# Two-layer hybrid decoder trunk: a third down block by Strassen's scheme, its weight sums partly on GpSimd, and the stick-breaking norm ahead of the query up-projection

## Chip, cores and metric

The kernel runs on one core of one Trainium2 chip. The metric is the time of one execution on the device, in microseconds (us). A core has TensorE (PE in the profile; its weight loads are PEld), VectorE (DVE), ScalarE (ACT), GpSimd (POOL) and SyncE (SP), which here only issues DMAs. PE writes its results to PSUM, eight banks of 128x512 f32; everything else lies in SBUF.

## The reference

256 tokens of width 1024 pass through two layers. A layer has two half-step SwiGLU feed-forwards (width 2816), between them a token mixer of two attention groups side by side, and at the end a gated input embedding. Cut to what matters:

```
h = h + 1/2 * swiglu(rms_norm(h))                     # silu(x Wg) * (x Wu), then Wd: 2816 -> 1024
u = norm(h) @ w_in                                    # sb q, k, v | q latent | kv latent | rope key
sb  = rms_norm(stick_breaking(q, k, v))               # 8 heads of 64
mla = rms_norm(softmax attention from the latents)    # q = norm(c_q) @ w_uq, kv = norm(c_kv) @ w_ukv
h = h + concat(sb, mla) @ w_out
h = h + 1/2 * swiglu(rms_norm(h))
h = h + sigmoid(norm(h) @ Wg) * (p[i] @ Wp)
```

All of it is in f32. The kernel gets near f32 accuracy from three matmuls on a rounded format: each operand is split into a high part (a rounded copy) and a low part (the rest), and high x high, high x low and low x high are summed (`mm3`, L220 to L225, lines L222, L223, L224 of the profile).

## The kernel before

**Weights.** Every weight comes once from HBM in pieces of 128x1024 f32 (512 KB), in the order of use. A piece passes four stations: a DMA from SP into one of six `raw` buffers, a rounded copy by ScalarE into one of six `wh` buffers (L132), the subtraction raw - wh by VectorE into one of six `wl` buffers (L133), and PE. So the splitting of a piece can start only when PE has done with the piece six places ahead. A plain piece of the feed-forward feeds 12 matmuls of 512 columns.

**Feed-forward (`ffn`, L470).** The 2816 inner columns are five blocks of 512 (0 to 4) and one of 256 (5). Gate and up products are made block by block; ScalarE makes the silu (L475), VectorE multiplies (L479), PE transposes (L450, tile `ft`) and both engines split the result into `f` (L455, L456). Which moment the transposes take in PE's order is set by a small planner: `soon` puts a step off by so many us of estimated PE time, `tick` runs what is due, `flush` runs all.

Then comes the down projection into four banks `d`. A plain block is 48 matmuls. Blocks 1 and 2 (`SEVEN`, L32) use Strassen's scheme in Winograd's form on a 2x2 split of the block: seven products of six matmuls instead of eight, 42 in place of 48. Its left operands are sums of the gated activations (`sums`, L410, made when the block's transposes are done: four VectorE sums and a split). Its right operands are sums of the four 128x1024 weight quarters b11, b12, b21, b22. In `Seven.operands` (L179) all four sums are made in place by VectorE (`add`, L169, tile `raw`, line L170), and each of the seven operands is copied by ScalarE (L175) and subtracted by VectorE (L176). The order is: the plain block 0 (two weight units, `head`), Strassen block 1, the plain block 5, Strassen block 2, then eight VectorE steps that combine the banks and add them to h (L559 to L567), and the plain blocks 3 and 4 (`lagging`, L365), in which the second half of the tokens runs three chunks behind the first, so that the first half's residual, norm and transposes lie beside the second half's matmuls.

**Mixer (`mix`, L573).** Stick-breaking attention of four head pairs (`sb_scores`, `sb_tail`, `sb_values`) is interleaved with the input projections. At the end the order on PE is: `sb_values(2)`, the query up-projection `uq` (48 matmuls of 256 columns, L716 to L720), `sb_values(3)`, then the norm of the stick-breaking output (`token_norm`, L724: squares by ScalarE, logarithm and exponential for the square root, five VectorE steps, result `on_sb`), `kn` and `vm`, the two MLA score steps, the transposes of `on_sb` (`turned`, L739, tile `yt_sb`), whose split gives the operand `y0h`, `y0l` (layer 0; `y1` in layer 1), and the output projection `wo` (L845 on), which begins with these. GpSimd has one product for the rope key (L685) and three for the query's rope (L758, L759, L765) in each layer, and nothing else of weight.

**Order on the engines.** The framework sorts the instructions of each engine by its own estimate of when they are ready, with the program's order as priority, and hands out buffers in the same way; on the chip each engine runs its list strictly in order.

Of the kernel before, what the change touches and what calls it, by code (L numbers as in the profile page):

```python
# [17 lines left out]
P = 128  # L18
T = 256
# [9 lines left out]
WARM = 11  # L29


SEVEN = (1, 2)  # L32

F_TAGS = ("sbq", "sbk", "v", "vm", "n0h", "n0l", "n1h", "n1l", "f4h", "f4l", "f5h", "f5l")

# [10 lines left out]
def trunk(ctx: ExitStack, tc: tile.TileContext, xT, xr, pT, w, gains, fgain, consts, out):  # L46
# [41 lines left out]
    def load_consts():  # L88
        c = tp.tile([P, 768], F32, tag="w2", name="c")[:, : 5 * P]
        after(nc.sync.dma_start(c, consts[:, 0 : 5 * P]), newest_load[0])  # L90
        after(nc.sync.dma_start(c_sb[:, P:], consts[:, C_FOLD:]), newest_load[0])
        nc.vector.tensor_copy(c_r, c)
# [16 lines left out]
    class Unit:  # L109


        def __init__(self, nk, cols=None, sub=1, cut=1, again=None):
            self.u = at[0] if again is None else again.u
            at[0] += again is None
            self.cols = cols or UNIT // nk
            self.per = max(1, PIECE // self.cols)
            self.sub, self.cut = sub, cut
            self.parts, self.here = {}, set()
# [35 lines left out]
    class Seven:  # L154

        def __init__(self):
            self.u = at[0]
            at[0] += 2  # L160
            self.raw = {}

        def load(self, i):
            r = raw_p.tile([P, PIECE], F32, tag="raw", name=f"raw7_{self.u}_{i}")
            newest_load[0] = nc.sync.dma_start(r, w[self.u + i // 2, :, i % 2 * PIECE : (i % 2 + 1) * PIECE])
            self.raw[i] = r
            return r

        def add(self, i, j):  # L169
            nc.vector.tensor_tensor(self.raw[i], self.raw[i], self.raw[j], ALU.add)  # L170

        def parts(self, i):
            r, name = self.raw[i], f"{self.u}_{i}_{next(ids)}"
# [5 lines left out]
        def operands(self):  # L179

            b11, b12, b21, b22 = range(4)
            self.load(b11)
            yield 1, self.parts(b11)
            self.load(b22)
            yield 3, self.parts(b22)
            self.load(b12)
            self.add(b11, b12)
            yield 5, self.parts(b11)
            self.load(b21)
            yield 2, self.parts(b21)  # L190
            self.add(b12, b22)
            yield 7, self.parts(b12)
            self.add(b11, b22)
            yield 6, self.parts(b11)
            self.add(b11, b21)
            yield 4, self.parts(b11)


    due = []
# [27 lines left out]
    def both(x, *ix):  # L227
        return tuple(t[ix] for t in x)
# [161 lines left out]
    class Gates:  # L390
# [19 lines left out]
        def sums(self, i):  # L410

            a, b = self.turned[i, 0], self.turned[i, 1]
            lo, hi = slice(0, 2), slice(2, 4)
            e = SEVEN.index(i)
            out = tuple(f_p.tile([P, 4, T], F32R, tag=f"s{e}{q}", name=f"s{q}_{self.tag}_{i}") for q in "hl")
            two = [wt(f"w{2 + k}", f"sum{k}_{self.tag}_{i}") for k in range(2)]
            s1, s2, s3, s4 = (two[k // 2][:, k % 2].rearrange("p (a b) -> p a b", a=2) for k in range(4))
            nc.scalar.copy(s3, b[:, lo])
            nc.vector.tensor_tensor(s1, s3, b[:, hi], ALU.subtract)
            nc.vector.tensor_tensor(s2, s1, a[:, lo], ALU.subtract)  # L420
            nc.vector.tensor_tensor(s3, a[:, lo], s3, ALU.subtract)
            nc.vector.tensor_tensor(s4, s2, a[:, hi], ALU.add)
            for k in range(2):
                sh, sl = both(out, slice(None), slice(2 * k, 2 * k + 2))
                nc.scalar.activation(sh, two[k], AF.Copy)
                nc.vector.tensor_tensor(sl, two[k], sh.bitcast(F32), ALU.subtract)
            self.s[i] = out
# [42 lines left out]
    def ffn(x, n, tag, gcol, between=None, feed=None):  # L470
# [13 lines left out]
        for i in range(NBLK):  # L484
            last = i == NBLK - 1
            g = [bank(f"g_{tag}_{i}{t}") for t in range(2)]
            sub = {"sub": 2} if feed and i == 0 else {}
            wg = wide([Unit(4, **sub) for _ in range(2)])
            if last:
                for k in range(KC):  # L490
                    for t in range(2):
                        tok_mm(g[t], wg, x, t, (k,))
                for t in range(2):
                    silu, rest = gated(i, t, g[t][:, 0:T], g[t][:, T : 2 * T], T)
                    rest()
                logs_after(silu)
                continue
            u = [bank(f"u_{tag}_{i}{t}") for t in range(2)]
            wu = wide([Unit(4, **sub) for _ in range(2)])
            if i == 0 and feed:  # L500
                for k in range(KC):
                    if k % 2 == 0:
                        feed(k // 2)
                    for o, w_of in ((g, wg), (u, wu)):
                        for t in range(2):
                            tok_mm(o[t], w_of, x, t, (k,))
                feed(4)
                first = [g, u]
                continue
            else:  # L510
                if i == 0:
                    tok_mm(g[0], wg, x, 0)
                    flush()
                    tok_mm(g[1], wg, x, 1)
                else:
                    for k in range(KC):
                        for t in range(2):
                            tok_mm(g[t], wg, x, t, (k,))
                if i == 1 and feed:
                    load_consts()  # L520
                    for t in range(2):
                        gated(0, t, first[0][t], first[1][t])[1](4.5)
                rests = [gated(i, t, g[t], u[t])[1] for t in range(2)]
                for k in range(KC):
                    for t in range(2):
                        tok_mm(u[t], wu, x, t, (k,))
            for r in rests:
                r()
        d = four(f"d_{tag}")

        def block(i):

            us = [Unit(2) for _ in range(2 if i < NBLK - 1 else 1)]
            return [(us[k // 2], k % 2, 4 * i + k) for k in range(2 * len(us))]
# [3 lines left out]
                for t in range(2):  # L538
                    down_mm(d, u, j, gates(k), gates.at(k), t, first and c == 0, False)

        head = block(0)
        plain(head[:2], True)
        flush()
        plain(head[2:])

        p = {2: d[0][0], 3: d[0][1], 4: d[1][0]}
        p.update((i, bank(f"p{i}_{tag}")) for i in (1, 5, 6, 7))
        own = (1, 5, 6, 7)
        for i in SEVEN:
            seven_mm(p, gates.seven(i), Seven().operands(), lambda q: q in own and i == SEVEN[0], lambda q: q in own and i == SEVEN[-1])  # L550
            if i == SEVEN[0]:
                plain(block(NBLK - 1))

        def to_h(t, f, src):
            c = half(f)
# [11 lines left out]
        to_h(1, 1, b)  # L567
        if between is not None:
            between()
        rest = [c for i in range(1, NBLK - 1) if i not in SEVEN for c in block(i)]  # L570
        return lagging(rest, d, gates, 0.5, tag, gcol, 3, False)

    def mix(x, n, L, g0):  # L573
# [136 lines left out]
        nc.tensor.matmul(f[:, :T], fold, krt, start=True, stop=True)  # L710
        kr = at_p.tile([P, T], F32, tag="kr", name=f"kr{L}")
        nc.vector.tensor_copy(kr, f[:, :T])
        sb_values(2)


        u = Unit(2)  # L716
        qs = [pair(f"uq{L}_{i}") for i in range(4)]
        for m in range(8):
            for k in range(2):
                mm3(qs[m // 2][:, m % 2], u.at(k, m * P, (m + 1) * P), both(xq, slice(None), k), k == 0, k == 1)  # L720

        sb_values(3)

        def token_norm(src, name):  # L724

            ss = tp.tile([P, 2], F32, tag="tss", name=f"tss_{name}")
# [12 lines left out]
        def turned(o, c0, gcol, name, parts=(0, 1)):  # L739

            for i in parts:
# [5 lines left out]
                for j in range(2):  # L747
                    c = 2 * i + j
                    split(y, a[:, j], c0 + c, gcol + c, name)

        y = new_x(f"y{L}")
        on = token_norm(ov, f"sb{L}")

        qn = at_p.tile([P, 4, T], F32, tag="sbq", name=f"qn{L}")
        for i in range(2):
# [62 lines left out]
        def mla_values(hp):  # L818
            pt = st["t", hp]
            for e in range(2):  # L820
# [3 lines left out]
                nc.tensor.matmul(om[1][:, c], pt[:, e, P:T], vm[:, 0, c], start=hd == 0, stop=True, skip_group_check=True)  # L824
                nc.tensor.matmul(om[1][:, c], pt[:, e, T:W], vm[:, 1, c], start=False, stop=True, skip_group_check=True)

        mla_scores(0)
        mla_scores(1)
        mla_probs(0)
        turned(on, 0, g0 + G_SB, f"sb{L}")  # L830
        mla_probs(1)
        nc.vector.reciprocal(ri, sm)
        d = four(f"wo{L}_")
# [141 lines left out]
def _weights(i):  # L975
# [9 lines left out]
    for L in range(DEPTH):  # L985
# [5 lines left out]
        def ffn(n):  # L991
            wg, wu, wd = (i[f"{n}_w_{s}"][L] for s in ("gate", "up", "down"))
            for j in range(NBLK - 1):
                m = ar(512 * j, 512 * j + 512)
                wide(wg, m)
                wide(wu, m)
            m = ar(DFF - 256, DFF)
            wide(np.concatenate([wg[:, m], wu[:, m]], axis=1), ar(512))

            def down(b):  # L1000
                units.extend(cols(wd[k : k + 256], ar(DM)) for k in range(512 * b, min(512 * b + 512, DFF), 256))

            down(0)
            for b in SEVEN:
                for k in (512 * b, 512 * b + 256):
                    units.append(np.concatenate([cols(wd[k : k + 256], ar(c, c + 512)) for c in (0, 512)], axis=1))
                if b == SEVEN[0]:
                    down(NBLK - 1)
            for b in range(1, NBLK - 1):
                if b not in SEVEN:  # L1010
                    down(b)
# [81 lines left out]
```

## Time and profile before

| | |
|---|---|
| three runs | 1039.70, 1041.15, 1043.06 us; median 1041.15 us |
| the profiled execution, by the clock of the runs | 1042.18 us |
| its span in the trace (first to last instruction) | 1040.3 us |
| busy: PE, PEld, DVE, ACT, POOL | 1019.1, 858.3, 714.9, 602.7, 7.3 us |
| mean granted PE clock | 0.992 |
| instructions | 13749, of them 5130 matmuls |
| read from HBM | 185.45 MB |

Times in the trace count from the span's start. A matmul's row shows its own duration from start to end; matmuls overlap in the array, so what one costs is the distance between two starts, and the rows below are used in that way. "idle before <- X" names what ended an engine's wait. Layer 0's first feed-forward (`a0` here, tiles `_a`) has its down projection from 132 to 191 us, its mixer follows until 300 us; the second feed-forward (`b0`) has its down projection from about 430 us. Layer 1 repeats this some 513 us later.

### The profile page before, as it was taken

To read this page: it belongs to the slowest core of one execution; us is meant where nothing else is said; L and a number is where in the kernel's file an instruction comes from. 1 tells how busy PE (TensorE), PEld (TensorE's weight loads), DVE (VectorE), ACT (ScalarE), POOL (GpSimd) and SP (SyncE) were. 2 spreads that over 40 slices of the span, in tenths; PEclk is the share of its full clock that TensorE was granted. 3 is DMA by queue.
4 is the path that set the end of the run, shared out by engine and by line. 5 is a ranking of instruction groups with operands and counts; after the bars stand their busy time and mean duration, and the time that the engine had idled before them with its cause. 6 is when DMAs were issued, how large, how long until landed. Compare 5 with 4: busy or idle time off the path is not lost.

```text
span 1040.3 us, 13749 instructions
## 1 busy us (share of the span) xinstructions
PE 1019.1 (98%) x5130; PEld 858.3 (82%) x5130; DVE 714.9 (69%) x991; ACT 602.7 (58%) x921; POOL 7.3 (1%) x13
## 2 busy tenths in 40 slices
PE   9999999999899999999999999999998999999996
PEld 8878888899788888877888888889997888888785
DVE  5676578866576665788875656888675756657975
ACT  5945455766565554555764555456855745545564
POOL 0000000000000000000000000000010000000000
PEclk9999999999899999999999999999999999999998
DMA  8865545763236555357565554476533365553551
GB/s 299 310 214 183 181 138 186 244 212 133 81 127 209 186 184 185 122 189 244 167 218 183 182 186 158 141 258 222 189 102 101 136 218 189 185 183 121 190 205 41
DMA packets 53490, 187.39 MB, mean 180 GB/s; under 512 B 6064, under 2 KB 6192, under 8 KB 53424
## 3 DMA queue, kind: packets, MB, share of 16 engines
q1 hardware_dynamic: 52992, 185.95, 53.1%
q8 instruction: 40, 0.66, 0.3%
q10 hardware_dynamic: 432, 0.57, 0.2%
q14 instruction: 26, 0.21, 0.1%
HBM read 185.45 MB, written 1.05 MB: 179 GB/s over the span
## 4 chain that ended last, share of the span: by engine, by line
PE 79%; DVE 9%; ACT 6%; issue 3%; DMA 2%; SPq 0%; ACTq 0%; DVEq 0%
PE g_b L224 4%; PE g_b L222 4%; PE g_b L223 4%; PE u_b L223 3%; PE u_b L224 3%; PE u_b L222 3%; PE g_a L224 3%; PE g_a L222 3%; PE g_a L223 3%; PE u_a L222 3%; PE u_a L223 3%; PE u_a L224 3%; DVE wl L176 3%; DVE raw L170 2%; PE d_a L223 2%
## 5 line engine op out<-in xcount | busy, mean ns | idle before, releaser
L133 DVE TENSOR_TENSOR wl<-raw,wh 128x1024 fp32r<-128x1024 f32 (+1 forms) x322 | 382.8, 1198 | 220.0 <-ACT wh L132 217.7
L132 ACT ACTIVATE wh<-raw 128x1024 fp32r<-128x1024 f32 (+1 forms) x322 | 330.1, 1037 | 251.8 <-PE u_b L224 50.2
L175 ACT ACTIVATE wh<-raw 128x1024 fp32r<-128x1024 f32 x56 | 58.0, 1057 | 63.5 <-DVE raw L170 37.3
L176 DVE TENSOR_TENSOR wl<-raw,wh 128x1024 fp32r<-128x1024 f32 x56 | 67.5, 1223 | 30.8 <-ACT wh L175 30.2
L223 PE MATMUL d_b<-wl,fh_b 128*128 128x512 f32 x128 | 50.7, 396 | 3.3 <-DVE wl L133 2.2
L223 PE MATMUL d_a<-wl,fh_a 128*128 128x512 f32 x128 | 50.0, 393 | 0.8 <-DVE wl L176 0.8
L224 PE MATMUL d_b<-wh,fl_b 128*128 128x512 f32 x128 | 50.0, 390 | 0.0
L224 PE MATMUL d_a<-wh,fl_a 128*128 128x512 f32 x128 | 49.6, 390 | 0.0
L222 PE MATMUL d_a<-wh,fh_a 128*128 128x512 f32 x128 | 49.0, 394 | 0.0
L222 PE MATMUL d_b<-wh,fh_b 128*128 128x512 f32 x128 | 48.4, 394 | 0.0
L170 DVE TENSOR_TENSOR raw<-raw,raw 128x1024 f32<-128x1024 f32 x32 | 39.1, 1221 | 0.6
L222 PE MATMUL g_a<-wh,x0h 128*128 128x512 f32 x96 | 38.5, 403 | 0.0
L222 PE MATMUL g_b<-wh,x_mix0h 128*128 128x512 f32 x96 | 38.4, 400 | 0.0
L222 PE MATMUL g_b<-wh,x_mix1h 128*128 128x512 f32 x96 | 38.4, 400 | 0.0
L222 PE MATMUL g_a<-wh,xe0h 128*128 128x512 f32 x96 | 38.4, 400 | 0.0
L224 PE MATMUL g_a<-wh,xe0l 128*128 128x512 f32 x96 | 37.6, 391 | 0.0
L224 PE MATMUL g_b<-wh,x_mix1l 128*128 128x512 f32 x96 | 37.5, 390 | 0.0
L224 PE MATMUL g_b<-wh,x_mix0l 128*128 128x512 f32 x96 | 37.5, 390 | 0.0
L223 PE MATMUL g_b<-wl,x_mix0h 128*128 128x512 f32 x96 | 37.4, 390 | 0.0
L223 PE MATMUL g_b<-wl,x_mix1h 128*128 128x512 f32 x96 | 37.4, 390 | 0.0
L223 PE MATMUL g_a<-wl,xe0h 128*128 128x512 f32 x96 | 37.4, 390 | 0.0
L223 PE MATMUL g_a<-wl,x0h 128*128 128x512 f32 x96 | 37.4, 391 | 0.0
(452 smaller groups left out, 2516.7 us busy)
## 6 DMA issues: line engine op xcount, KB each, us to landing
raw<-in_w SPq DMA_DIRECT2D x338, 512.0 KB, 4.1
raw<-in_w SPq DMA_DIRECT2D x16, 256.0 KB, 4.6
xin<-in_xT SPq DMA_DIRECT2D x4, 256.0 KB, 4.9
h<-in_xr SPq DMA_DIRECT2D x2, 512.0 KB, 7.9
p<-in_pT SPq DMA_DIRECT2D x2, 256.0 KB, 6.2
fg<-in_fgain SPq DMA_DIRECT2D x1, 512.0 KB, 7.1
out_h<-hg SPq DMA_DIRECT2D x2, 256.0 KB, 2.3
out_h<-hg ACTq DMA_DIRECT2D x2, 256.0 KB, 2.7
```

What stands on the lines that cost most here:

```text
L132: nc.scalar.activation(wh[:, a], r[:, a], AF.Copy),
L133: nc.vector.tensor_tensor(wl[:, a], r[:, a], wh[:, a].bitcast(F32), ALU.subtract),
L170: nc.vector.tensor_tensor(self.raw[i], self.raw[i], self.raw[j], ALU.add)
L175: newest_wh[0] = nc.scalar.activation(wh, r, AF.Copy)
L176: nc.vector.tensor_tensor(wl, r, wh.bitcast(F32), ALU.subtract)
L222: nc.tensor.matmul(o, ah, bh, start=start, stop=False, **kw)
L223: nc.tensor.matmul(o, ah, bl, start=False, stop=False, **kw)
L224: newest_mm[0] = nc.tensor.matmul(o, al, bh, start=False, stop=stop, **kw)
```

## The change

Four edits. (1) Block 3 joins the Strassen blocks. The order becomes: half of block 0, Strassen 1, the other half of block 0, Strassen 2, block 5, Strassen 3, the combination, block 4. (2) Of the four weight sums of a Strassen block two go to GpSimd (b12 + b22, and b11 + that sum), two stay on VectorE. The products are taken in the order 1, 3, 2, 7, 6, 5, 4. The activation sums of blocks 1 and 2 lie in one of the two x buffers, those of block 3 in the buffers `s0h`, `s0l`, which block 1 used before. The weights of block 4 are asked for ahead of the combination (`u.ready()`). (3) In the mixer `sb_values(3)` and the norm come before `uq`, and the transposes of `on_sb` before the MLA scores. (4) In the very first feed-forward the silu of block 0 is ordered behind the exponential of the second token half's norm.

```diff
-SEVEN = (1, 2)
+SEVEN = (1, 2, 3)
...
+        def sum(self, eng, o, a, b, op=ALU.add):
+            eng.tensor_tensor(self.raw[o], self.raw[a], self.raw[b], op)
...
             self.load(b11)
             yield 1, self.parts(b11)
+            self.load(b12)
             self.load(b22)
+            self.sum(nc.gpsimd, b12, b12, b22)
             yield 3, self.parts(b22)
-            self.load(b12)
-            self.add(b11, b12)
-            yield 5, self.parts(b11)
+            self.sum(nc.gpsimd, b11, b11, b12)
             self.load(b21)
             yield 2, self.parts(b21)
-            self.add(b12, b22)
             yield 7, self.parts(b12)
-            self.add(b11, b22)
             yield 6, self.parts(b11)
-            self.add(b11, b21)
-            yield 4, self.parts(b11)
+            self.sum(nc.vector, b22, b11, b22, ALU.subtract)
+            yield 5, self.parts(b22)
+            self.sum(nc.vector, b21, b11, b21)
+            yield 4, self.parts(b21)
...
+            if e == 0:
+                self.spare = tuple(x_p.tile([P, KC, T], F32R, tag=f"x{q}", name=f"sx{q}_{self.tag}") for q in "hl")
+            if e < 2:
+                out = both(self.spare, slice(None), slice(4 * e, 4 * e + 4))
+            else:
+                out = tuple(f_p.tile([P, 4, T], F32R, tag=f"s0{q}", name=f"s{q}_{self.tag}_{i}") for q in "hl")
...
+                    exp = newest[0]
                     for t in range(2):
-                        gated(0, t, first[0][t], first[1][t])[1](4.5)
+                        silu, r = gated(0, t, first[0][t], first[1][t])
+                        after(silu, exp)
+                        r(4.5)
...
         plain(head[:2], True)
         flush()
-        plain(head[2:])
...
-            if i == SEVEN[0]:
-                plain(block(NBLK - 1))
+            if i != SEVEN[-1]:
+                plain(head[2:] if i == SEVEN[0] else tail)
+
+        rest = [c for i in range(1, NBLK - 1) if i not in SEVEN for c in block(i)]
+        for u, _, _ in rest[::2]:
+            u.ready()
...
-        sb_values(2)
-        u = Unit(2)
-        qs = [pair(f"uq{L}_{i}") for i in range(4)]
-        for m in range(8):
-            for k in range(2):
-                mm3(qs[m // 2][:, m % 2], u.at(k, m * P, (m + 1) * P), both(xq, slice(None), k), k == 0, k == 1)
-        sb_values(3)
...
+        sb_values(2)
+        sb_values(3)
         y = new_x(f"y{L}")
         on = token_norm(ov, f"sb{L}")
+        u = Unit(2)
+        qs = [pair(f"uq{L}_{i}") for i in range(4)]
+        for m in range(8):
+            for k in range(2):
+                mm3(qs[m // 2][:, m % 2], u.at(k, m * P, (m + 1) * P), both(xq, slice(None), k), k == 0, k == 1)
...
+        turned(on, 0, g0 + G_SB, f"sb{L}")
         mla_scores(0)
         mla_scores(1)
         mla_probs(0)
-        turned(on, 0, g0 + G_SB, f"sb{L}")
```

The packing of the weights follows the new order.

More of the change, by code (lines that the diff above doesn't have):

```diff
@@ L163, in load @@
         def load(self, i):
[L164 to L170, printed above, removed]
+            self.raw[i] = raw_p.tile([P, PIECE], F32, tag="raw", name=f"raw7_{self.u}_{i}")
+            newest_load[0] = nc.sync.dma_start(self.raw[i], w[self.u + i // 2, :, i % 2 * PIECE : (i % 2 + 1) * PIECE])
+        def sum(self, eng, o, a, b, op=ALU.add):
+            eng.tensor_tensor(self.raw[o], self.raw[a], self.raw[b], op)
         def parts(self, i):
@@ L414, in sums @@
             e = SEVEN.index(i)
-            out = tuple(f_p.tile([P, 4, T], F32R, tag=f"s{e}{q}", name=f"s{q}_{self.tag}_{i}") for q in "hl")
+            if e == 0:
[4 more added lines that the diff above has]
+                out = tuple(f_p.tile([P, 4, T], F32R, tag=f"s0{q}", name=f"s{q}_{self.tag}_{i}") for q in "hl")
             two = [wt(f"w{2 + k}", f"sum{k}_{self.tag}_{i}") for k in range(2)]
@@ L539, in plain @@
                     down_mm(d, u, j, gates(k), gates.at(k), t, first and c == 0, False)
-        head = block(0)
+        head, tail = block(0), block(NBLK - 1)
         plain(head[:2], True)
         flush()
-        plain(head[2:])
         p = {2: d[0][0], 3: d[0][1], 4: d[1][0]}
@@ L569, in ffn @@
             between()
-        rest = [c for i in range(1, NBLK - 1) if i not in SEVEN for c in block(i)]
         return lagging(rest, d, gates, 0.5, tag, gcol, 3, False)
@@ L1003, in ffn @@
             down(0)
+            down(NBLK - 1)
             for b in SEVEN:
@@ L1006, in ffn @@
                     units.append(np.concatenate([cols(wd[k : k + 256], ar(c, c + 512)) for c in (0, 512)], axis=1))
-                if b == SEVEN[0]:
-                    down(NBLK - 1)
             for b in range(1, NBLK - 1):
```

## The prediction

> **What bounds the kernel now.** I read the page first, then the waits of PE, then the stages in which PE waits (windows and timeline).
>
> ```profile
> PE 1019.1 (98%) x5130; PEld 858.3 (82%) x5130; DVE 714.9 (69%) x991; ACT 602.7 (58%) x921; POOL 7.3 (1%) x13
> ...
> PEclk9999999999899999999999999999999999999998
> ```
>
> PE is busy nearly all the time, and its granted clock falls below full in one slice in the middle (the eleventh, 260 to 286 us). A busy PE could still be a slow one, so its pace has to be read from the distance of two starts. These are the first and the last of the 42 matmuls of Strassen block 1 and the first one behind them:
>
> ```profile
> 143.71 0.39 PE L222 MATMUL p_a<-wh,fh_a 128*128 128x512 f32 x1
> ...
> 153.22 0.39 PE L222 MATMUL d_a<-wh,fh_a 128*128 128x512 f32 x1
> ```
>
> 42 matmuls in 9.51 us are 0.2265 us each, and no wait lies between them. So in the feed-forwards PE itself is the bound: fewer matmuls help there as long as VectorE and ScalarE keep up. All of PE's waits, but for one at the very start, are these:
>
> ```profile
> PE wo L222 <- ACT y0h L267: 2.8, 1, 2.8
> PE wo L222 <- ACT y1h L267: 2.8, 1, 2.8
> PE d_b L223 <- DVE wl L133: 2.2, 2, 1.1
> PE ft_a L450 <- DVE pr_a L479: 1.2, 1, 1.2
> PE d_b L223 <- DVE wl L176: 1.1, 2, 0.7
> PE d_a L223 <- DVE wl L176: 0.8, 2, 0.4
> ```
>
> Two are the output projection `wo`, one in each layer, which stands until the stick-breaking operand is split. 2.2 + 1.1 + 0.8 = 4.1 us are at the end of the Strassen blocks, where VectorE's subtraction comes late. 1.2 us is in the first feed-forward. The two waits for `wo` cost more than their length:
>
> ```profile
> 271.03:273.87 2.84, 0.00 (x0) 0.00 (x0) 1.36 (x8) 2.84 (x12) 0.00 (x0) 0.88 0.21 79
> 273.87:279.16 5.29, 5.29 (x12) 4.02 (x13) 2.03 (x5) 2.65 (x11) 0.00 (x0) 0.50 0.00 0
> 787.08:791.10 4.02, 4.02 (x13) 3.08 (x13) 2.04 (x5) 2.65 (x11) 0.00 (x0) 0.69 0.00 0
> ```
>
> (Columns: stretch and length; busy time and count of PE, PEld, DVE, ACT, POOL; granted clock; DMA.) After the idle stretch the clock is at 0.50 and the first 12 matmuls of `wo` take 5.29 us; in layer 1 they take 4.02 us at 0.69. At 12 x 0.2265 = 2.72 us that is 2.57 + 1.30 = 3.9 us lost to the clock.
>
> **The change: the mixer.** The chain behind the wait, by the timelines of PE, ACT and DVE in layer 0:
>
> ```profile
> 254.80 0.36 PE L222 MATMUL uq<-xqs0l,wh 128*128 128x256 f32 x1
> 260.64 0.33 PE L634 MATMUL ov<-v,a 128*128 128x64 f32 x2
> 264.80 0.38 PE L789 MATMUL s<-kn,qn 128*128 128x128 f32 x2
> 270.00 1.03 PE L746 MATMUL yt_sb<-c_sb,on_sb 128*128 128x128 f32 x8
> 251.40 1.06 ACT L626 ACTIVATE a<-z 128x384 f32<-128x384 f32 x2 [0.20 <-PE z L625]
> 260.36 2.01 ACT L132 ACTIVATE wh<-raw 128x1024 fp32r<-128x1024 f32 x2 [4.96 <-PE uq L223]
> 262.27 0.58 ACT L729 ACTIVATE junk_sb<-ov 128x512 f32<-128x512 f32 x1
> 268.16 1.39 DVE L735 TENSOR_SCALAR on_sb<-ov,tss_sb 128x512 f32<-128x512 f32 x2
> ```
>
> `sb_values(3)` needs the exponential that ends at 252.46, so nothing holds it at 254.80: it moves ahead by 260.64 - 254.80 = 5.8 us, and `uq` goes back by its length. ScalarE is idle for 4.96 us just there, so the squares can start at 262.27 - 5.8 = 256.4. From the squares to the end of `on_sb` the chain took 269.55 - 262.27 = 7.3 us, with other VectorE work in between; taken whole, `on_sb` would be ready at 263.7. PE comes to its transposes, now ahead of the scores, at 264.80: 1.1 us to spare. The scores then end at 271.03, and the split of `y0` has had their 5.2 us as cover. So I let both waits go, 2 x 2.84 = 5.7 us, and with them the half clock, 3.9 us. Nothing is added in instructions; POOL's and SP's lists are passed by no new step.
>
> What is late next is the MLA softmax, which is also 1.03 us later, behind the transposes:
>
> ```profile
> 275.89 0.54 ACT L807 ACTIVATE ex<-s,nb 128x256 f32<-128x256 f32 x1
> 279.16 1.90 PE L815 MATMUL pt<-c_sb,ex 128*128 128x128 f32 x12
> ```
>
> The last exponential ends 2.7 us before PE asks for it. `wo` would now start at 271.03 and PE would ask at 271.03 + 2.72 = 273.75, which is 5.4 us earlier, while the exponentials lose the four copies of `y0h` that lay among them and some 2.4 us of norm work on VectorE ahead of them (1.39 for `on_sb`, 0.86 and 0.15 in rows below). I take 0.5 us of new wait in each layer, 1.0 in all, between 0 and 2.7 each.
>
> **The first feed-forward.** ScalarE reloads its tables between the two halves of the norm:
>
> ```profile
> 37.95 1.28 ACT L280 ACT_TABLE_LOAD   x1
> 43.26 1.28 ACT L475 ACT_TABLE_LOAD   x1
> ```
>
> With the silu behind the second exponential these two loads of 1.28 us go, and a third just before. Weight copies wait behind them in ScalarE's list, the subtractions and products of VectorE behind these, and the 1.2 us of PE ends on such a product (`pr_a`). I let it go: 1.2 us, between 0 and 1.2. The first silu waits a little longer; its cover is the estimate of 4.5 us that the planner gives its transposes.
>
> **The third Strassen block.** Six matmuls less in each of four feed-forwards: 24 x 0.2265 = 5.4 us. The added activation sums (four of VectorE and a split, for block 3) fall into the gate and up products, where PE takes 12 x 0.2265 = 2.72 us for a piece and VectorE one subtraction (1.22, below); they cost nothing. The moved units (half of block 0, block 5) issue the same loads in another order. In the second feed-forwards the load of `p` now waits until the third block has used `s0h`, and behind it in SP's list are weights of the embedding; both are wanted only after the eight half chunks of block 4, 8 x 6 x 0.2265 = 10.9 us, which covers the load.
>
> The open price is GpSimd. Its sum of 1024 columns is not in the trace; these are the nearest rows, with what VectorE did beside them:
>
> ```profile
> 715.33 0.73 POOL L685 TENSOR_TENSOR rk<-r_a,c_sb 128x256 f32<-128x256 f32 x1 [449.73 <-ACT r_a L324]
> 264.32 1.28 POOL L765 TENSOR_TENSOR qr<-r,r 128x512 f32<-128x512 f32 x1 [5.22 <-DVE tss_sb L287]
> 713.78 1.22 DVE L133 TENSOR_TENSOR wl<-raw,wh 128x1024 fp32r<-128x1024 f32 x1
> 715.44 1.71 DVE L133 TENSOR_TENSOR wl<-raw,wh 128x1024 fp32r<-128x1024 f32 x1
> 264.76 0.86 DVE L281 TENSOR_TENSOR tss_sb<-tss_sb,y_sb 128x2 f32<-128x2 f32 x1
> 266.69 0.15 DVE L282 SCALAR_TENSOR_TENSOR tss_sb<-tss_sb,y_sb 128x2 f32<-128x2 f32 x1
> ```
>
> By columns, 0.73 and 1.28 us go on to 1.28 + 2 x 0.55 = 2.4 us. And the two engines do not run side by side: a VectorE step on two columns, which takes 0.15 us, took 0.86 and ended at 265.62, where POOL's ended (265.60); a subtraction of 1.22 us took 1.71 and had its last 1.08 us behind POOL's end (716.06). All of VectorE's steps in a Strassen block have two inputs in SBUF, as these two had. So a sum on GpSimd can cost VectorE 2.4 us where it cost 1.13 before. The Trainium skill says the same ("SBUF — State Buffer", Who interferes with whom): a VectorE instruction with two SBUF inputs and a GpSimd instruction that reads SBUF exclude each other for the whole instruction, whichever starts first; it speaks against this part of the change, and the rows agree.
>
> ```profile
> 152.15 2.35 DVE L176 TENSOR_TENSOR wl<-raw,wh 128x1024 fp32r<-128x1024 f32 x2
> DVE wl L176 <- ACT wh L175: 7.5, 6, 1.5
> raw<-in_w SPq DMA_DIRECT2D x338, 512.0 KB, 4.1
> ```
>
> Queued subtractions follow each other in 2.35 - 1.22 = 1.13 us. The run of three Strassen blocks with two plain units has 3 x 9 + 4 = 31 VectorE steps, 35.0 us, and six GpSimd sums, 14.4 us: 49.4 us, if they exclude each other. PE needs (3 x 42 + 48) x 0.2265 = 39.4 us. The deficit of 10.0 us meets two credits. The first block's two sums, 4.8 us, run while VectorE waits for free buffers (7.5 us of such idle time from 130 to 168 us); and VectorE starts six products ahead, 6 x 1.36 = 8.2 us. By this ledger 3.0 us are left over and PE never waits. But a block is also a chain: GpSimd sum, copy (1.0, by the row above with two in 2.01), subtraction, VectorE sums. I walked it with these prices. The second block ends 1.7 us ahead of PE. Its fifth product's quarter frees the buffer for b22 of the third at -9.7 us (0 is PE's start of block 3), and 4.1 us later it has landed. The first GpSimd sum ends at -2.8, three subtractions hold the second until 0.6, it ends at 3.0, two sums and the subtraction of product 6 end at 6.4, and PE wants that at 4 x 1.36 = 5.4: a wait of 1.0 us, or 1.8 if the subtraction goes ahead of the two sums. Between 0 and 1.8 I take 1.2 us a feed-forward, nearer to the walk.
>
> The second new squeeze is the end of the stage:
>
> ```profile
> 170.95 0.68 DVE L564 TENSOR_TENSOR a_a<-p_a,u_a 128x512 f32<-128x512 f32 x1
> 171.55 0.68 DVE L556 SCALAR_TENSOR_TENSOR h<-v_a,h 128x512 f32<-128x512 f32 x1
> 184.75 0.69 DVE L359 SCALAR_TENSOR_TENSOR h<-d_a,h 128x512 f32<-128x512 f32 x1 [1.08 <-PE d_a L224]
> 192.00:205.00 13.00, 12.90 (x81) 11.08 (x81) 12.61 (x29) 9.97 (x25) 0.73 (x1) 1.00 0.64 198
> ```
>
> Combination steps follow each other in 0.60 us, and the first half's residual came at 184.75, ten us after them. Now only four chunks follow the Strassen blocks. VectorE, done with product 4 at 8.7 in the walk, has four subtractions (4.5) and eight steps (4.8) to do, until 18.0; the residual is due at 9.5 + 1.0 + 5.4 = 15.9. It is 2.1 us late, under 5.4 us of second-half matmuls, and what follows (192 to 205) has VectorE busy for 12.61 of 13.00 us, so part of it may come back. Between 0 and 2.1 I take 0.6 us.
>
> The 4.1 us of old waits go, since the weights of block 4 are now asked for ahead of the combination; what is late in their place is the 1.8 us above.
>
> **Sum.** Gains: 5.7 + 3.9 + 1.2 + 5.4 + 4.1 = 20.3 us. New waits: 4 x 1.8 + 1.0 = 8.2 us. Net -12.1: the profiled execution of 1042.18 us (span 1040.3 and 1.9 around it) would be 1030.1, and the median, 1.03 below it, 1029.
>
> **The rivals.** (a) GpSimd and VectorE fit beside each other, or GpSimd's sums all fall into idle time: 8.2 less 1.0 of new waits go, 1041.15 - 19.3 = 1022. For it speaks the ledger, against it the two held VectorE steps. (b) The norm is not early enough: VectorE's list puts weight subtractions between its steps, and PE waits at the transposes or for the softmax instead, with the clock falling again. Up to 5.7 + 3.9 come back: 1029 to 1039. The 1.1 us to spare is thin; the light VectorE load before 261 us speaks against it. (c) Slower: the exclusion closes a ring. Buffer freed, load (4.1), two GpSimd sums (4.8), VectorE sum, copy and subtraction (3.4) are 12.3 us, and with two plain and three other subtractions in between (5.7) 18.0 us, against PE's 15.0 us for a block and a unit. Three turns are 54 us against 39.4 + 8.2: 6.4 us of wait a feed-forward, and a wait of 2.84 us was enough for the half clock, 1.3 to 2.57 us more. At 4 x 8.3 us the sum is -20.3 + 1.0 + 33 = +14: 1055. It decides from 4.8 us of new waits a feed-forward on. Against it: in the walk five subtractions of the ring run while loads and sums do.
>
> **How the numbers follow.** Forecast 0.53, (a) 0.20, (b) 0.14, (c) 0.07, others 0.06. 0.3%, about what a measurement can tell from no change here, is 3.1 us: faster means below 1038.0. The forecast, (a) and most of (b) lie there: 0.86; same 0.07; slower 0.07. The forecast's own range is 1024 to 1034 (new waits of 0.4 to 3.0 a feed-forward); 1020 to 1037 takes in (a) and most of (b).
>
> **What would show it.** Right: no wait of `wo` for `y0h`, `y1h`; the clock at 1.00 around 270 and 780; 12 `wo` matmuls in 2.7 us; 24 matmuls less; POOL's sums near 2.4 us with VectorE steps stretched beside them; PE waits of about 1 us on L176 in the third Strassen block. Wrong: PE waiting on `yt_sb` or `pt`, a second clock dip, or waits over 3 us a feed-forward in the down stages.

## The result, and the profile after

The changed kernel takes 1051.78 us (median of 4 runs, 1050.5 to 1055.56) against 1041.02 us before (4 runs, 1039.7 to 1043.06): ratio 1.0108, 95% interval 1.0077 to 1.0139. It is slower by about 10.8 us, where 12.1 us of gain were forecast. The profiled execution has 1051.31 us, span 1049.5.

From the page of the kernel after, the busy times:

```profile
PE 1015.4 (97%) x5106; PEld 853.0 (81%) x5106; DVE 746.4 (71%) x1019; ACT 618.6 (59%) x942; POOL 77.8 (7%) x37
```

The 24 matmuls are gone (5106 for 5130) and PE's busy share still fell. Half of the answer is in the mixer, and there the forecast came true. PE's timeline in layer 0:

```profile
268.86 1.04 PE L745 MATMUL yt_sb<-c_sb,on_sb 128*128 128x128 f32 x8
...
274.94 0.40 PE L221 MATMUL wo<-wh,y0h 128*128 128x512 f32 x1
275.18 0.40 PE L222 MATMUL wo<-wl,y0h 128*128 128x512 f32 x1
```

Neither row ends in a bracket, so PE waited for neither; `wo` follows the scores, and two of its matmuls start 0.24 us apart, not at half clock. The other half is in the list of PE's waits, all in feed-forwards (its line 223 of before is now 222, 450 is 455):

```profile
PE xt_b L332 <- DVE h L358: 8.8, 2, 4.5
PE xt_a L332 <- DVE h L358: 5.0, 3, 2.4
PE d_a L222 <- DVE wl L175: 2.6, 2, 1.7
PE d_b L222 <- DVE wl L175: 2.0, 2, 1.3
PE ft_a L455 <- DVE pr_a L484: 1.8, 2, 1.0
PE ft_b L455 <- DVE pr_b L484: 1.2, 1, 1.2
...
PE p_b L222 <- DVE wl L175: 0.8, 2, 0.4
PE p_a L222 <- DVE wl L175: 0.7, 2, 0.3
```

These eight rows are 22.9 us, 5.7 a feed-forward. The largest, 13.8 us, stand at the transposes `xt` of the first half of h, behind the residual on VectorE (`h`, L358), at the end of the down stage. The clock falls at three of them (columns: stretch and length; busy time and count of PE, PEld, DVE, ACT, POOL; granted clock; DMA):

```profile
189.70:193.20 3.50, 3.50 (x14) 2.91 (x14) 3.10 (x7) 2.89 (x9) 0.00 (x0) 0.54 0.63 197
486.70:490.20 3.50, 2.71 (x10) 2.32 (x11) 3.50 (x5) 2.54 (x6) 0.00 (x0) 0.54 0.47 153
1002.10:1009.00 6.90, 4.55 (x15) 3.86 (x16) 5.99 (x10) 2.90 (x7) 0.00 (x0) 0.52 0.51 156
```

At granted clocks of 0.54, 0.54 and 0.52 PE's 3.50, 2.71 and 4.55 us of matmuls in these stretches lose 1.6 + 1.2 + 2.2 = 5.0 us. (In the rest of the second and the third stretch, 0.8 and 2.35 us, PE still stands; the eight rows have that already. In the third the clock fell before the wait was over.) So 27.9 us of new losses stand against the gains. GpSimd's sums and VectorE's subtractions in Strassen blocks, as groups:

```profile
L169 POOL TENSOR_TENSOR raw<-raw,raw 128x1024 f32<-128x1024 f32 x24 | 66.5, 2770 | 720.5 <-DMA raw<-in_w 694.9 <-DVE wl L175 22.7 <-issue 2.4
...
L175 DVE TENSOR_TENSOR wl<-raw,wh 128x1024 fp32r<-128x1024 f32 x84 | 114.4, 1388 | 28.4 <-ACT wh L174 27.2
L169 DVE TENSOR_TENSOR raw<-raw,raw 128x1024 f32<-128x1024 f32 x24 | 29.4, 1224 | 18.8 <-POOL raw L169 18.3
```

A GpSimd sum takes 2.77 us in the mean, and 2.40 where nothing holds it (the first one of the program, below). VectorE's subtractions rose to 1.39 us, and VectorE stands 18.3 us at its own sums for GpSimd's. In the third block of the first feed-forward both are seen; VectorE's timeline, and GpSimd's below it, with that first sum ahead:

```profile
165.63 2.44 DVE L175 TENSOR_TENSOR wl<-raw,wh 128x1024 fp32r<-128x1024 f32 x1 [2.50 <-ACT wh L174]
170.35 1.23 DVE L169 TENSOR_TENSOR raw<-raw,raw 128x1024 f32<-128x1024 f32 x1 [2.28 <-POOL raw L169]
```

```profile
117.28 2.40 POOL L169 TENSOR_TENSOR raw<-raw,raw 128x1024 f32<-128x1024 f32 x1 [116.35 <-DMA raw<-in_w]
...
164.59 5.73 POOL L169 TENSOR_TENSOR raw<-raw,raw 128x1024 f32<-128x1024 f32 x2 [12.95 <-DMA raw<-in_w]
```

The two GpSimd sums run from 164.59 to 170.32. In that time VectorE finishes one subtraction of 1.22 us, stretched to 2.44, and then stands for the second sum.

### The profile page after: what moved, and what is told of

It reads as the page before. It is cut to its first block, busy times and chain, and to the rows that moved or that the text cites. A ratio compares the mean times of both kernels' runs of the same rounds, so it can differ in the third digit from the quotient of the medians.

```text
span 1049.5 us, 13812 instructions
## 1 busy us (share of the span) xinstructions
PE 1015.4 (97%) x5106; PEld 853.0 (81%) x5106; DVE 746.4 (71%) x1019; ACT 618.6 (59%) x942; POOL 77.8 (7%) x37
## 4 chain that ended last, share of the span: by engine, by line
PE 74%; DVE 9%; DMA 5%; ACT 4%; issue 4%; POOL 4%; POOLq 0%; SPq 0%; ACTq 0%; DVEq 0%
DVE wl L175 4%; PE g_b L223 4%; PE g_b L221 4%; PE g_b L222 4%; POOL raw L169 4%; PE g_a L223 3%; PE g_a L221 3%; PE g_a L222 3%; PE u_b L223 3%; PE u_b L221 3%; PE u_b L222 3%; PE u_a L222 3%; DMA raw<-in_w 3%; PE u_a L223 3%; PE u_a L221 3%
## 5 line engine op out<-in xcount | busy, mean ns | idle before, releaser
L133 DVE TENSOR_TENSOR wl<-raw,wh 128x1024 fp32r<-128x1024 f32 (+1 forms) x306 | 369.3, 1216 | 185.0 <-ACT wh L132 181.2
L132 ACT ACTIVATE wh<-raw 128x1024 fp32r<-128x1024 f32 (+1 forms) x306 | 314.0, 1037 | 203.3 <-PE u_b L223 50.2
L174 ACT ACTIVATE wh<-raw 128x1024 fp32r<-128x1024 f32 x84 | 88.8, 1061 | 87.2 <-DMA raw<-in_w 19.9
L175 DVE TENSOR_TENSOR wl<-raw,wh 128x1024 fp32r<-128x1024 f32 x84 | 114.4, 1388 | 28.4 <-ACT wh L174 27.2
L169 POOL TENSOR_TENSOR raw<-raw,raw 128x1024 f32<-128x1024 f32 x24 | 66.5, 2770 | 720.5 <-DMA raw<-in_w 694.9
L222 PE MATMUL d_a<-wl,fh_a 128*128 128x512 f32 x104 | 41.4, 398 | 2.6 <-DVE wl L175 2.6
L222 PE MATMUL d_b<-wl,fh_b 128*128 128x512 f32 x104 | 41.7, 401 | 2.0 <-DVE wl L175 2.0
L169 DVE TENSOR_TENSOR raw<-raw,raw 128x1024 f32<-128x1024 f32 x24 | 29.4, 1224 | 18.8 <-POOL raw L169 18.3
L223 PE MATMUL d_b<-wh,fl_b 128*128 128x512 f32 x104 | 41.2, 397 | 0.0
L223 PE MATMUL d_a<-wh,fl_a 128*128 128x512 f32 x104 | 41.0, 394 | 0.0
```

What stands on the lines that cost most here:

```text
L132: nc.scalar.activation(wh[:, a], r[:, a], AF.Copy),
L133: nc.vector.tensor_tensor(wl[:, a], r[:, a], wh[:, a].bitcast(F32), ALU.subtract),
L169: eng.tensor_tensor(self.raw[o], self.raw[a], self.raw[b], op)
L174: newest_wh[0] = nc.scalar.activation(wh, r, AF.Copy)
L175: nc.vector.tensor_tensor(wl, r, wh.bitcast(F32), ALU.subtract)
L222: nc.tensor.matmul(o, ah, bl, start=False, stop=False, **kw)
```

## Experiments

**Theories.** X: a GpSimd step that reads SBUF and a VectorE step with two inputs in SBUF exclude each other, so a sum on GpSimd takes from VectorE up to its own 2.4 us, where VectorE would do it in 1.2. S: VectorE and the copies stand for GpSimd's results because of the order of their lists; with another order the two would run side by side. T: the third block with only four chunks behind it is too much, whichever engine adds. P: the transposes stand too early in PE's list.

**The parts by themselves.** `e1_mixer` is the kernel before with the mixer edit and the silu order alone; `e2_down` is the kernel before with the rest of the diff alone.

> The kernel before with only the mixer edit and the order of the first silu; the down blocks as before. In the trace after, PE's excess over its ideal pace fell in the two mixers from 18.7 to 13.7 and from 17.2 to 13.0 us, and the wait of 1.2 us in the first feed-forward is gone. If these are gains that stand by themselves, 9.2 + 1.2 = 10.4 us: 1041 - 10.4 = 1030.6 (1029 to 1033). Rival: part of them only came because the feed-forward ahead ended late, so that weights were loaded ahead; then under half stays, 1036 or more.

1030.83 us, ratio 0.9897 (0.9882 to 0.9913): 10.6 us, as expected.

> The kernel before with only the down blocks changed (three Strassen blocks, half of the weight sums on GpSimd). If the parts add up, 1051.8 + 10.4 = 1062 (1059 to 1064), with PE waits at the transposes of h behind the residual in all four feed-forwards and the clock at about 0.5 behind the long ones. Rival: the two parts get in each other's way (the mixer's earlier end moves loads into the feed-forward's front); then the down part alone costs less, 1046 to 1055.

1061.09 us, ratio 1.0185 (1.0165 to 1.0205). The parts add up: the mixer and silu give 10.6 us, and the down blocks cost 19.6 us alone and 1051.78 - 1030.83 = 21.0 us with the mixer in place.

**Which part of the down blocks.** `e3_vector` puts GpSimd's two sums back on VectorE, in three Strassen blocks:

```diff
-            self.sum(nc.gpsimd, b12, b12, b22)
+            self.sum(nc.vector, b12, b12, b22)
...
-            self.sum(nc.gpsimd, b11, b11, b12)
+            self.sum(nc.vector, b11, b11, b12)
```

> The kernel after with all four weight sums of a block on VectorE and nothing on GpSimd. Theory G, GpSimd is the cause (VectorE is held by its sums or stands for them, some 18 us in the trace after): most of the 22.9 us of PE waits and 6.8 us of half clock go, against 24 more sums of 1.13 us on VectorE, part of them in idle time; 1026 to 1038. Theory T, the third block with only four chunks behind it is the cause, whichever engine adds: VectorE ends its list as late as before or later, PE stands at the transposes for 2.4 to 4.5 us as in the kernel after; 1047 to 1060.

1022.52 us, ratio 0.9816 (0.9798 to 0.9833): 29.3 us faster than the change, faster than both kernels, and below even the range of theory G. What is left of the eight rows above:

```profile
PE xt_b L332 <- DVE h L358: 1.0, 1, 1.0
PE xt_a L332 <- DVE h L358: 0.7, 1, 0.7
```

T falls. The third block with its short tail runs when VectorE does everything. `e4_two` is the change with two Strassen blocks:

```diff
-SEVEN = (1, 2, 3)
+SEVEN = (1, 2)
...
-            if i != SEVEN[-1]:
-                plain(head[2:] if i == SEVEN[0] else tail)
+            if i == SEVEN[0]:
+                plain(head[2:] + tail)
```

> The kernel after with two Strassen blocks, 1 and 2, so that eight chunks in place of four follow them; half of the sums still on GpSimd. 24 matmuls come back (5.4 us). Theory T, the short end of the stage is the cause: no wait at the transposes of h, no half clock behind it, only waits of about 1 us in the products; 1030.6 with the mixer's gain alone, within 3 us of that. Theory G, GpSimd's sums are the cause: two thirds of the 29.7 us stay, 1042 to 1050.

1028.49 us, ratio 0.9875 (0.9858 to 0.9891), the number of T, though T had just fallen: GpSimd's 16 sums did not cost two thirds of 29.3 us. `e9_two_vector` has these two blocks with all sums on VectorE:

> Two Strassen blocks and eight chunks behind them, as in the run of 1028.5 us, but with all sums on VectorE. If GpSimd's sums are dear only where VectorE has no slack left (three blocks): the same within 2 us, 1026.5 to 1030.5. If each GpSimd sum costs its share of the 29.3 us that lie between the kernel after and the one with everything on VectorE, 16 of 24 sums give 19 us: 1009; PE's matmuls alone forbid that (24 more than in the 1022.5 us run, which has 2 us of waits), so the floor is 1025.

1025.03 us, ratio 0.9839 (0.9824 to 0.9854). 16 GpSimd sums cost 3.5 us in two blocks, 0.2 each (a little more than I allowed for "the same"), and 24 cost 29.3 in three, 1.2 each. What differs is VectorE's free time. The same 40 us of the down stage of the first feed-forward in `e9_two_vector` and `e4_two` (two blocks), then in `e3_vector` and in the kernel after (three):

```profile
143.00:183.00 40.00, 40.00 (x179) 33.11 (x178) 31.32 (x33) 19.71 (x21) 0.00 (x0) 1.00 0.64 223
```

```profile
143.00:183.00 40.00, 40.00 (x178) 33.14 (x177) 31.02 (x30) 19.80 (x21) 5.67 (x2) 1.00 0.64 226
```

```profile
143.00:183.00 40.00, 40.00 (x178) 33.14 (x177) 38.78 (x39) 22.25 (x23) 0.00 (x0) 1.00 0.65 226
```

```profile
143.00:183.00 40.00, 38.00 (x167) 30.75 (x166) 32.58 (x28) 21.40 (x22) 12.30 (x4) 1.00 0.53 173
```

With two blocks VectorE has 8.7 us free in 40, and with GpSimd's two sums beside it PE still loses nothing. With three blocks it is busy for 38.78 and does 39 steps, and PE loses nothing here either. In the kernel after it does 28 steps in that time while GpSimd does four sums: eleven steps less, of which only four are the sums that GpSimd took over. No run varies the free time alone; the two blocks also have eight chunks behind them in place of four.

**Is it the order, or exclusion?** `e7_order` puts VectorE's two sums behind the subtraction of product 7, so that VectorE does what is free before it stands (`after` orders two steps without a wait):

```diff
             yield 7, self.parts(b12)
+            sub7 = self.sub
             yield 6, self.parts(b11)
-            self.sum(nc.vector, b22, b11, b22, ALU.subtract)
+            after(self.sum(nc.vector, b22, b11, b22, ALU.subtract), sub7)
             yield 5, self.parts(b22)
-            self.sum(nc.vector, b21, b11, b21)
+            after(self.sum(nc.vector, b21, b11, b21), sub7)
```

> The kernel after with VectorE's two sums put behind the subtraction of product 7 in its list, which needs only the first GpSimd sum; nothing else changes. In the trace after VectorE stands 8 times for 2.3 us, 18.3 us in all, at such a sum for the second GpSimd sum, with free subtractions behind it. Theory S, this standing is the cause: most of the 18.3 us come back on VectorE and with them the waits of PE at the transposes; 1028 to 1040. Theory X, GpSimd's sum and a VectorE step with two inputs in SBUF exclude each other, so that the 2.4 us of a GpSimd sum are lost to VectorE whether it stands or is held: the standing turns into stretched subtractions; 1045 to 1055.

1054.65 us, ratio 1.0124 (1.0098 to 1.015): nothing gained. Its groups on VectorE:

```profile
L175 DVE TENSOR_TENSOR wl<-raw,wh 128x1024 fp32r<-128x1024 f32 x84 | 128.6, 1567 | 30.6 <-ACT wh L174 30.3
L169 DVE TENSOR_TENSOR raw<-raw,raw 128x1024 f32<-128x1024 f32 x24 | 28.2, 1213 | 0.0
```

The standing at L169 went from 18.8 to 0.0 us, and the subtractions rose from 114.4 to 128.6: the wait turned into stretched steps, as X has it. So S falls for the order of VectorE's list; the copies' place was not changed here. `e8_beside` takes all standing for GpSimd away: it keeps VectorE's list of `e3_vector` step for step and gives GpSimd work that nobody waits for:

```diff
+        def beside(self, i):
+            nc.gpsimd.tensor_tensor(self.scratch, self.raw[i], self.raw[i], ALU.add)
...
+            self.beside(b22)
             self.sum(nc.vector, b12, b12, b22)
...
             self.sum(nc.vector, b11, b11, b12)
+            self.beside(b11)
```

> All four sums of a block on VectorE, with VectorE's list the same step for step as in the run with everything on VectorE (1022.5 us), and beside it GpSimd adds one of the same weight buffers to itself, 128 x 1024, at the two places where it added before, into a buffer that nobody reads. So GpSimd does the work of the kernel after, and nobody waits for its result. Theory S (the waits for GpSimd's result are the cause): 1021 to 1027. Theory X (exclusion): VectorE loses up to 24 x 2.4 = 58 us and still has the 24 sums of 1.2 us; at or above the kernel after, 1050 to 1085, with subtractions of 1.2 us stretched to 2 to 3.6 us beside GpSimd.

1065.65 us, ratio 1.0235 (1.0209 to 1.026): 43.1 us lost to 24 GpSimd steps for whose result nothing waits, 1.8 each. GpSimd's timeline, and VectorE's below it:

```profile
145.82 2.23 POOL L166 TENSOR_TENSOR beside<-raw 128x1024 f32<-128x1024 f32 x1 [15.85 <-DMA raw<-in_w]
152.69 2.74 POOL L166 TENSOR_TENSOR beside<-raw 128x1024 f32<-128x1024 f32 x1 [4.63 <-DVE raw L173]
```

```profile
146.22 2.92 DVE L173 TENSOR_TENSOR raw<-raw,raw 128x1024 f32<-128x1024 f32 x1
...
151.33 1.21 DVE L173 TENSOR_TENSOR raw<-raw,raw 128x1024 f32<-128x1024 f32 x1
152.46 4.04 DVE L179 TENSOR_TENSOR wl<-raw,wh 128x1024 fp32r<-128x1024 f32 x2
```

A VectorE sum of 1.21 us takes 2.92 beside GpSimd and ends 1.09 us behind GpSimd's end (149.14 and 148.05), as the held subtraction in the prediction did (1.08). So S falls altogether. This step lost 1.7 us. In the whole kernel, by the pages of `e3_vector` and `e8_beside`, the same 1043 steps of VectorE became 38.9 us longer, 1.6 for each GpSimd step, and the kernel lost 43:

```profile
PE 1006.8 (99%) x5106; PEld 849.2 (83%) x5106; DVE 752.4 (74%) x1043; ACT 617.8 (61%) x942; POOL 7.4 (1%) x13
PE 1018.8 (96%) x5106; PEld 851.8 (80%) x5106; DVE 791.3 (74%) x1043; ACT 617.2 (58%) x942; POOL 68.3 (6%) x37
```

Could it be that GpSimd's read kept a weight buffer from being refilled? `e11_const` reads two columns of the weight buffer as a trigger and then adds the constants:

```diff
+            nc.gpsimd.tensor_tensor(self.scratch[:, :2], self.raw[i][:, :2], self.raw[i][:, :2], ALU.add)
+            nc.gpsimd.tensor_tensor(self.scratch, c_sb[:, :PIECE], c_sb[:, :PIECE], ALU.add)
```

> As the run with GpSimd's idle work beside an all-VectorE list (1065.7 us), but at the same two places GpSimd reads two columns of the weight buffer, as a trigger, and then adds the 1024 columns of constants to themselves, into the buffer that nobody reads. So it holds no weight buffer. Theory X (exclusion, whatever buffer is read): 1058 to 1072. Rival B, the 43 us were lost because GpSimd's read kept weight buffers from being refilled: 1022 to 1030.

1062.35 us, ratio 1.0205 (1.0174 to 1.0235). Rival B falls: which buffer is read makes no difference clear of the noise. `e12_memset` has the same trigger and then writes zeros in place of adding:

```diff
-            nc.gpsimd.tensor_tensor(self.scratch, c_sb[:, :PIECE], c_sb[:, :PIECE], ALU.add)
+            nc.gpsimd.memset(self.scratch, 0.0)
```

> The same trigger of two columns, and then GpSimd writes zeros to the 1024 columns and reads nothing from SBUF. If only a GpSimd step that reads SBUF keeps VectorE out: the two-column steps alone remain, 1022 to 1030, and no VectorE step of 1.2 us is stretched to 2 us or more beside the write. If any GpSimd step does: stretched steps as before, 1045 to 1070.

1024.27 us, ratio 0.9837 (0.9819 to 0.9855), which overlaps the interval of `e3_vector`. GpSimd's and VectorE's timelines:

```profile
144.45 0.96 POOL L167 MEMSET beside<- 128x1024 f32 x1
149.03 1.04 POOL L166 TENSOR_TENSOR beside<-raw 128x2 f32<-128x2 f32 x1 [3.62 <-DVE raw L174]
150.12 0.96 POOL L167 MEMSET beside<- 128x1024 f32 x1
```

```profile
144.25 1.22 DVE L174 TENSOR_TENSOR raw<-raw,raw 128x1024 f32<-128x1024 f32 x1
...
148.79 2.35 DVE L180 TENSOR_TENSOR wl<-raw,wh 128x1024 fp32r<-128x1024 f32 x2
```

The write of 144.45 lies wholly inside a VectorE sum, and that takes its 1.22 us. VectorE's subtractions in the Strassen blocks take 1.22 us in the mean, against 1.38 in `e11_const`. So GpSimd holds VectorE by reading SBUF, not by working. The Trainium skill says just this ("SBUF — State Buffer", Who interferes with whom): VectorE with two SBUF inputs contends with a GpSimd instruction that reads SBUF, not with one that only writes it.

`e10_one` is the change with only the second sum (`b11`) back on VectorE: 12 GpSimd sums.

> The kernel after with only the first sum of a block on GpSimd, the second back on VectorE: 12 GpSimd sums. Theory S: nobody stands for the first sum in the trace after but a copy, so nearly all is back: 1022 to 1027. Theory X: VectorE has 12 sums of 1.2 us more than in the kernel after and is held for 12 x 2.4 us less, net 14 us of VectorE time in the whole kernel or 3.6 us a feed-forward; PE's waits of 7.4 us a feed-forward fall by up to that: 1030 to 1042.

1042.18 us, ratio 1.0009 (0.9993 to 1.0024), 0.2 us past the upper end of X and far from S: 19.7 us above `e3_vector`, 1.6 a sum. It does not price a sum cleanly, because VectorE now also stands for that first sum:

```profile
DVE raw L169 <- POOL raw L169: 16.8, 5, 5.7
```

**The place of the transposes, and p.** `e5_later` puts the first half's transposes further back in PE's list:

```diff
+        wait = (1.2, 1.9) if first else (3.4, 3.9)
...
-                        residual(nx, nn, d, t, scale, tag, gcol)
+                        residual(nx, nn, d, t, scale, tag, gcol, wait if t == 0 else (1.2, 1.9))
```

> The kernel after with the transposes of the first half of h, at the end of a feed-forward, put later in PE's list: 3.4 and 3.9 us of products behind the residual in place of 1.2 and 1.9. Theory X (VectorE is late as a whole): PE waits less at these transposes, but their splits come later too and PE waits at the next stage's first products instead; 1046 to 1054. Rival P, the place is the cause: the 13.8 us of waits at the transposes and the 6.8 us of half clock behind them go, 1032 to 1040.

1056.7 us, ratio 1.015 (1.0131 to 1.0168), slower than the change, past either range. PE's waits of this kernel:

```profile
PE xt_b L332 <- DVE h L358: 7.8, 4, 2.8
PE d_a L222 <- DVE wl L175: 4.1, 2, 2.9
...
PE v L221 <- ACT x_a1h L266: 2.1, 1, 2.1
...
PE v L223 <- DVE x_a1l L267: 1.6, 2, 1.0
PE v L223 <- DVE x_a0l L267: 1.3, 2, 0.7
```

In part the waits moved to the next stage's products (`v`), in part they stayed at the transposes. P falls: VectorE is late as a whole. These rows do not account for all of the 4.9 us by which the run is slower than the change. `e6_p` gives the embedding input p and its two parts buffers that the third block doesn't use:

```diff
-        pr = at_p.tile([P, 4, T], F32, tag="s0h", name=f"p{L}")[:, 0:2]
+        pr = at_p.tile([P, 4, T], F32, tag="s1l", name=f"p{L}")[:, 0:2]
...
-        xp = tuple(at_p.tile([P, 4, T], F32R, tag=g, name=f"xp{g}{L}")[:, 0:2] for g in ("s0l", "s1h"))
+        xs = at_p.tile([P, 4, T], F32R, tag="s1h", name=f"xp{L}")
+        xp = xs[:, 0:2], xs[:, 2:4]
```

> The kernel after with the embedding input p and its two parts in buffers that the third Strassen block doesn't use (s1l and the two halves of s1h), so that the load of p needn't wait for that block. In the trace after VectorE stands 1.5 us for it ahead of the residual in the second feed-forwards, where PE's wait at the transposes is 4.5 us against 2.4 in the first. If that stand is the difference: 2 x 2.1 us of wait and some 3 us of half clock go, 1043 to 1047. If VectorE's other work sets the end: 1050 to 1053.

1045.49 us, ratio 1.004 (1.0024 to 1.0056): 6.3 us better than the change, as expected.

```profile
PE xt_a L332 <- DVE h L358: 5.0, 3, 2.4
PE xt_b L332 <- DVE h L358: 4.7, 2, 2.4
```

The second feed-forwards now wait as the first do: 4.7 us in place of 8.8.

## Why the prediction was wrong, point by point

**Right.** The mixer was to give 5.7 + 3.9 - 1.0 and the silu order 1.2, 9.8 us in all; alone they measured 10.6. The 24 matmuls are gone, and so are the old waits of 4.1 us (none of their rows is left in `e9_two_vector` or `e3_vector`). From `e1_mixer` to `e9_two_vector`, both with two Strassen blocks and nothing on GpSimd, are 5.8 us, for these waits and the new order together.

**The price of a GpSimd sum** was right as a duration: 2.4 us forecast, 2.40 measured where nothing holds it. What it took from VectorE is less in the mean. Without 24 sums of 1.21 us VectorE's busy time should have fallen by 29.1 us from `e3_vector`'s 752.4; it fell to 746.4, so the other steps were stretched by 23.1 us. With the 18.3 us of standing for GpSimd's sums these are 41.4 us, 1.7 a sum, and 12.3 us more than VectorE was relieved of. That 24 x (2.4 - 1.2) = 28.8 us is nearly the 29.3 us between the change and `e3_vector` is therefore luck: PE lost more than VectorE did, some of it to the half clock and to the load of p below. What was wrong is what became of the price.

**The step that failed** is the second squeeze, at the end of the stage: "2.1 us late, under 5.4 us of second-half matmuls", taken at 0.6 us a feed-forward. The trace has 13.8 us of PE's waits at the transposes and 5.0 us of half clock at them, 18.8 / 4 = 4.7 us a feed-forward. In the first feed-forward VectorE came to the residual here:

```profile
188.78 1.28 DVE L358 SCALAR_TENSOR_TENSOR h<-d_a,h 128x512 f32<-128x512 f32 x2
```

That is 20.8 us behind PE's start of block 3 (168.01), against 18.0 in the walk. VectorE was done with product 4 at 178.39, 10.4 in place of 8.7, and had five subtractions, not four, between that and the residual. Three more errors are in the step:
- Its cover. I counted the second half's products, but the transposes stand in PE's list only six matmuls (1.4 us) behind the last product of the first half; these are the first and the last of the six, after which PE stands until 189.52. More cover alone does not save it: `e5_later` gave it, and PE waited in the next stage.

```profile
185.64 0.39 PE L221 MATMUL d_a<-wh,fh_a 128*128 128x512 f32 x1
...
186.78 0.39 PE L223 MATMUL d_a<-wh,fl_a 128*128 128x512 f32 x1
```

- The ledger ahead of it. Its deficit was 10.0 us a feed-forward, against credits of 4.8 + 8.2. If that deficit stands, PE's waits of 5.7 us a feed-forward leave 4.3 us for the two credits together. I read both as work done ahead of time, which moves VectorE's lateness to the end of the stage and does not remove it; no run shows this by itself. The first block's two GpSimd sums, which were to run in VectorE's idle time, were not free either: `ft` waits are 3.0 us, 0.75 a feed-forward, and `e3_vector` has none. Which credit was over by how much was not measured.
- The load of p. I covered it by 10.9 us of PE's matmuls, but PE was not the one to wait: VectorE stood for it (for ScalarE's copy of it, `xps0l`) ahead of the residual in its list. `e6_p` prices that at 6.3 us, 3.1 in each second feed-forward.

```profile
484.40 0.69 DVE L891 TENSOR_TENSOR xps1h<-p,xps0l 128x512 fp32r<-128x512 f32 x1 [1.46 <-ACT xps0l L890]
```

**The third block** itself came out near the walk in size, 1.2 us a feed-forward against (2.6 + 2.0 + 0.8 + 0.7) / 4 = 1.5 us, but for the most part not in place, so the size is partly luck. The walk has PE wait at product 6, the fifth; there it waited (0.8 + 0.7) / 4 = 0.4 us. The other 1.15 us came at product 2, the third (in the first feed-forward until 172.77): its subtraction stood in VectorE's list behind the sum that waited 2.28 us for GpSimd. The softmax wait of 1.0 us did not come.

Together 1.2 + 0.6 = 1.8 us a feed-forward were 1.5 + 0.75 + 4.7 = 6.95. 4 x 5.15 = 20.6 us are most of the 22.8 us from 1029 to 1051.8; the rest was not traced. Rival (c) had the size (8.3 us a feed-forward, 1055) and exclusion as its ground, but not the place: no ring closes in the products (1.5 us, not 6.4), the lateness is paid at the end. Its chance of 0.07 rested on the walk. VectorE's 49.4 us of work for 39.4 us of PE should have weighed more than a walk; but such a count does not give the size, for by the same prices `e3_vector` has 37 steps, 41.8 us, for 39.4, and PE waits only 1.7 us at its transposes in the whole kernel.

The best version measured is `e3_vector`: the whole change but for GpSimd, 1022.5 us, 1.8% faster than before.

## What to carry to other kernels

Before work is moved from VectorE to GpSimd, look at what VectorE does meanwhile: if its steps have two inputs in SBUF and the moved one reads SBUF, VectorE can lose up to GpSimd's duration: here 1.7 us in the mean for a sum that takes GpSimd 2.40 us, and VectorE itself 1.2. In none of these runs did the move pay; it cost 0.2 us a sum with 8.7 of 40 us free, and 1.2 us a sum with 1.2 of 40 free. Where an engine is over its budget in a stage, do not count on work done ahead to pay the debt, for here the debt came due at the stage's end; the step to watch there is the first one on another engine that waits for that engine's list.

## What was unexpected in the hardware

- VectorE at 38.78 of 40 us, with 39 steps, cost PE nothing in that time and 0.7 us at the transposes behind it (`e3_vector`): an engine that is nearly full need not be late, but it had no room for GpSimd's sums.
- A GpSimd add of one buffer to itself cost VectorE 1.7 us at 1024 columns (a step of 1.21 us became 2.92), and takes 1.89 us where nothing holds it, against 2.40 for a sum of two buffers; a GpSimd write of 1024 columns took 0.96 us and cost it nothing.
- The exclusion works the other way too: in `e12_memset` the two-column GpSimd step of 149.03 starts 0.24 us after a VectorE subtraction, takes 1.04 us and ends at 150.07, where that subtraction ends (148.79 + 1.22 = 150.01); where nothing holds it, such a step takes 0.19 us (at 127.54).
- The same wait halved the clock once and once not. In the kernel after, PE stands 2.35 us in layer 0 and 2.38 us in layer 1 at the same transposes; behind the first lies the stretch at 0.54 shown above, around the second the clock is 1.00 (timeline of PE, then the window). Why one and not the other was not found.

```profile
189.52 0.70 PE L332 MATMUL xt_a<-c_sb,h 128*128 128x128 f32 x4 [2.35 <-DVE h L358]
...
706.52 0.66 PE L332 MATMUL xt_a<-c_sb,h 128*128 128x128 f32 x4 [2.38 <-DVE h L358]
```

```profile
703.00:716.00 13.00, 10.33 (x54) 8.07 (x53) 12.38 (x25) 9.03 (x24) 0.00 (x0) 1.00 0.72 255
```
